# A scan kernel's last tile: one load in 32 KiB pieces in place of four loads in 2 KiB pieces, and three stores in place of four

## The chip, the cores and the metric

The kernel runs on one core of a Trainium2 chip. Times are device microseconds of one execution, unprofiled runs and a profiled one alike; the profile's *span* (from the first to the last recorded instruction of one profiled execution) is about 2 us shorter than the time.

The parts of a core that matter: TensorE (PE), VectorE (DVE), ScalarE (ACT), SyncE (SP, which here only issues loads), and 16 DMA engines that move all data between the chip's memory (HBM) and the on-chip memory (SBUF).

## The reference

`x` is 8 x 4096 x 2048 float32. Along the axis of 4096 the result is a running log-sum-exp:

```python
out[:, 0, :] = x[:, 0, :]
for t in range(1, S):
    mx = np.maximum(out[:, t-1, :], x[:, t, :])
    out[:, t, :] = mx + np.log(np.exp(out[:, t-1, :] - mx) + np.exp(x[:, t, :] - mx))
```

So 268.44 MB are read and 268.44 MB written, once each.

## The kernel before

A tile is 512 steps of one batch: 128 partitions, 4 successive rows each, 2048 columns. That is 4 MiB, and 32 KiB without a gap in HBM for each partition. There are 64 tiles, numbered 0 to 63 below, and five buffers. The columns of a tile are worked in four pieces of 512: ACT takes Exp, PE makes the prefix sums over the partitions, DVE adds the rows, ACT takes Ln. "Load 63" and "store 62" are the transfers of those tiles.

```python
    def load(b, k):
        t = iopool.tile([P, R, D], f32, name=f"io_{b}_{k}", tag="io")   # 5 buffers
        io[b, k] = t
        if (b, k) == tiles[-1]:
            for c in range(NC):                  # last tile: four column parts, runs of 2 KiB
                nc.sync.dma_start(out=t[:, :, cols(c)], in_=x_v[b, k][:, :, cols(c)])
        else:
            nc.sync.dma_start(out=t, in_=x_v[b, k])          # runs of 32 KiB
    ...
    def front(b, k, c):
        if c == 0:
            load(b, k)
        ...
        nc.scalar.activation(et, t[:, :, cols(c)], ACT.Exp)
    ...
    def back(b, k, c):
        t = io[b, k]
        nc.scalar.activation(t[:, :, cols(c)], sums.pop((b, k, c)), ACT.Ln)
        if (b, k) == tiles[-1]:
            nc.scalar.dma_start(out=o_v[b, k][:, :, cols(c)], in_=t[:, :, cols(c)])
        elif c == NC - 1:
            nc.scalar.dma_start(out=o_v[b, k], in_=t)

    for n, piece in enumerate(pieces):           # Ln of a piece comes two pieces after its Exp
        front(*piece)
        if n >= 1:
            carry(*pieces[n - 1])
        if n >= LAG:
            back(*pieces[n - LAG])
```

The softmax here doesn't subtract the row's maximum and nothing guards it: scores larger than these inputs give would overflow.

## Time and profile before

Median of four runs: 1259.86 us (1259.71 to 1260.11). The page of the profile begins so: the span, the busy time of each engine, the DMA share in 40 slices of the span (9 is 90% or more), and GB/s per slice:

```profile
span 1257.9 us, 5492 instructions
PE 638.5 (51%) x1472; PEld 215.0 (17%) x1472; DVE 703.3 (56%) x1024; ACT 930.0 (74%) x513; POOL 1.5 (0%) x10
DMA  9999999999999999999999999999999999999997
...
io<-in_x_dram SPq DMA_DIRECT2D x63, 4096.0 KB, 31.4
out_dram<-io ACTq DMA_DIRECT2D x63, 4096.0 KB, 38.5
io<-in_x_dram SPq DMA_DIRECT2D x4, 1024.0 KB, 39.4
out_dram<-io ACTq DMA_DIRECT2D x4, 1024.0 KB, 10.3
```

No compute engine is near full, and the DMA engines are: the kernel is bound by DMA. The last four lines are the DMA issues (number, size of one, median us from issue to landing).

The tail, in the timeline (start us, us, engine, line, operation, and in brackets how long the engine had been idle and what ended that):

```profile
1188.89 35.31 SPq L74 DMA_DIRECT2D io<-in_x_dram  x4
...
1199.57 24.63 SPq L74 DMA_DIRECT2D io<-in_x_dram  x1
...
1227.33 1.91 ACT L88 ACTIVATE et<-io 128x2048 bf16<-128x2048 f32 x1 [10.77 <-DMA io<-in_x_dram]
...
1234.67 0.34 ACTq L114 DMA_DIRECT2D out_dram<-io  x1
1246.97 0.54 ACTq L112 DMA_DIRECT2D out_dram<-io  x1
```

These are the four load issues of tile 63 (SP is held in them until 1224.2), its first Exp, the issue of store 62, and the last column store. The stretches view of the same time (stretch, length, busy us of each engine, TensorE clock, DMA share, GB/s):

```profile
1188.00:1202.00 14.00, 8.97 (x22) 3.02 (x21) 10.94 (x16) 14.00 (x8) 0.00 (x0) 0.80 1.00 422
1202.00:1220.00 18.00, 8.97 (x28) 3.11 (x27) 13.38 (x20) 14.55 (x9) 0.00 (x0) 1.00 1.04 431
1220.00:1236.00 16.00, 5.36 (x10) 1.76 (x10) 4.25 (x7) 8.67 (x5) 0.00 (x0) 0.57 0.48 183
1236.00:1258.00 22.00, 2.89 (x8) 0.78 (x7) 7.10 (x11) 9.55 (x6) 0.00 (x0) 0.54 0.91 358
```

From 1220 to 1236 the DMA engines are busy for 48%: 8.3 us of idle time for each engine *on average*.

The trace records when each DMA engine reports its share of a transfer as done, 16 reports for one transfer. I sorted these and took the median, the second latest and the latest engine (us; computed from the completion records, not a view of the profile):

```
before           median   second latest   latest    latest - median
tile  5 loaded     67.95        68.16       68.81       0.86
store 58         1180.23      1186.58     1188.84       8.61
store 60         1209.47      1213.33     1215.98       6.51
store 61         1223.58      1224.23     1226.36       2.78
load 63, part 4  1228.97      1232.42     1235.23       6.26
store 62         1245.86      1245.99     1246.59       0.73
last store       1256.73      1256.83     1256.95       0.22
```

One engine falls behind by some 8 us in the course of the run. All engines carry the same bytes of the tiles, and in the steady part none of them is idle. Others can run ahead because loads and stores are queued in advance. A tile is landed, and a buffer is free, only when the *latest* engine has reported. "DMA: Bandwidth & Descriptors" of the Trainium skill (Why a DMA increments its semaphore by 16 and not by 1) says the same: only the full count of 16 means that all data landed. The trace agrees: the next load is issued at 1188.89, 0.05 us after the latest engine's report for store 58, and 8.66 us after the median one's.

Besides the tiles, the DMA engines carry small transfers of the kind "instruction", which the page of the profile lists by queue (queue, kind: packets, MB, share of the engines' time):

```profile
q8 instruction: 11, 0.18, 0.1%
q14 instruction: 20, 0.16, 0.0%
```

In the steady part a packet starts when the one before it on its engine ends, so the packets of one engine can be followed as a chain. The chain of the latest engine holds eleven 8 KiB packets of queue 14, one about every 100 us from 57.8 to 1093.2 us; no other chain holds more than four. Each of them, with the stretched 32 KiB packet behind it (1.75 to 1.85 us in place of 1.21), costs the engine 0.85 to 0.94 us, 9.9 us together. Its other 32 KiB packets start every 1.210 us, as on the engines that are not late. The lag grows in steps, each after such a packet, and between the steps it is flat or falls (us; computed from the packet and completion records, not a view):

```
instruction packet at    latest - median before it    after it
 258.1                   1.75 (store 10)              2.76 (store 11)
 468.1                   3.58 (store 21)              4.49 (store 22)
 670.8                   4.23 (store 31)              5.19 (store 32)
 880.8                   6.00 (store 42)              6.97 (store 43)
1093.2                   7.79 (store 53)              8.75 (store 54)
```

So the latest engine is not slow as such: it has extra packets to carry. No run here changed the number of these packets, so this rests on the traces alone. The second latest engine is another case: its 32 KiB packets start every 1.219 us, and why stays open.

### The profile page before, as it was taken

To read this page: it belongs to the slowest core of one execution; us is meant where nothing else is said; L and a number is where in the kernel's file an instruction comes from. 1 tells how busy PE (TensorE), PEld (TensorE's weight loads), DVE (VectorE), ACT (ScalarE), POOL (GpSimd) and SP (SyncE) were. 2 spreads that over 40 slices of the span, in tenths; PEclk is the share of its full clock that TensorE was granted. 3 is DMA by queue.
4 is the path that set the end of the run, shared out by engine and by line. 5 is a ranking of instruction groups with operands and counts; after the bars stand their busy time and mean duration, and the time that the engine had idled before them with its cause. 6 is when DMAs were issued, how large, how long until landed. Compare 5 with 4: busy or idle time off the path is not lost.

```text
span 1257.9 us, 5492 instructions
## 1 busy us (share of the span) xinstructions
PE 638.5 (51%) x1472; PEld 215.0 (17%) x1472; DVE 703.3 (56%) x1024; ACT 930.0 (74%) x513; POOL 1.5 (0%) x10
## 2 busy tenths in 40 slices
PE   3655445544455455554556545455555454554542
PEld 1211112111111111111111111111111111111110
DVE  3665556565565554555555656565465555555453
ACT  5987768668677686776867768678687686776665
POOL 0000000000000000000000000000000000000000
PEclk9888688785887857878577786787767878678695
DMA  9999999999999999999999999999999999999997
GB/s 400 433 429 431 432 432 433 432 432 433 433 434 433 429 433 433 432 433 432 432 433 432 433 432 433 432 433 433 434 433 432 434 433 431 433 433 433 433 381 299
DMA packets 22399, 537.22 MB, mean 427 GB/s; under 512 B 2144, under 2 KB 2144, under 8 KB 6240
## 3 DMA queue, kind: packets, MB, share of 16 engines
q1 hardware_dynamic: 11184, 268.44, 49.7%
q10 hardware_dynamic: 11184, 268.44, 49.6%
q8 instruction: 11, 0.18, 0.1%
q14 instruction: 20, 0.16, 0.0%
HBM read 268.44 MB, written 268.44 MB: 427 GB/s over the span
## 4 chain that ended last, share of the span: by engine, by line
DMA 69%; ACT 14%; DVE 5%; PE 5%; issue 5%; SPq 1%; ACTq 0%; DVEq 0%
DMA io<-in_x_dram 67%; ACT io L110 8%; ACT et L88 5%; DVE st L98 4%; PE ps L91 3%; DMA out_dram<-io 2%; PE ps L103 2%; DVE st L96 1%; SPq L74 1%; ACTq L114 0%; ACTq L110 0%; DVEq L98 0%; ACTq L88 0%; DVEq L96 0%; SPq L76 0%
## 5 line engine op out<-in xcount | busy, mean ns | idle before, releaser
L88 ACT ACTIVATE et<-io 128x2048 bf16<-128x2048 f32 x256 | 485.3, 1897 | 301.1 <-DMA io<-in_x_dram 301.1
L98 DVE TENSOR_TENSOR st<-st,et 128x512 f32<-128x512 f32 x768 | 530.9, 692 | 43.4
L110 ACT ACTIVATE io<-st 128x2048 f32<-128x2048 f32 x256 | 484.6, 1894 | 15.0 <-DMA io<-in_x_dram 10.7
L96 DVE COPY st<-ps 128x512 f32<-128x512 f32 x256 | 176.7, 690 | 498.3 <-PE ps L91 492.9
L103 PE MATMUL ps<-st,last 128*128 128x512 f32 x448 | 304.6, 769 | 137.8 <-DVE st L98 136.6
L91 PE MATMUL ps<-et,Li 128*128 128x512 bf16 x256 | 124.9, 488 | 465.7 <-ACT et L88 463.9
L91 PE MATMUL ps<-et,Ls 128*128 128x512 bf16 x768 | 287.8, 497 | 0.0
L91 PEld LDWEIGHTS <-Ls 128*128 128x128 bf16 x768 | 89.4, 116 | 697.7 <-issue 668.1
L103 PEld LDWEIGHTS ps<-st,last 128*128 128x128 f32 x448 | 94.7, 234 | 250.8 <-DVE st L98 228.3
L91 PEld LDWEIGHTS <-Li 128*128 128x128 bf16 x256 | 30.8, 120 | 77.6 <-issue 70.2
L29 ACT ACT_TABLE_LOAD x1 | 1.3, 1283 | 0.8 <-PEq L138 0.8
masks.py:66 POOL TENSOR_SCALAR_AFFINE_SELECT Ls<-Ls 128x128 bf16<-128x128 bf16 x1 | 0.3, 293 | 0.0
L47 POOL TENSOR_SCALAR_AFFINE_SELECT last<-last 128x128 f32<-128x128 f32 x1 | 0.3, 292 | 0.1
masks.py:66 POOL TENSOR_SCALAR_AFFINE_SELECT Li<-Li 128x128 bf16<-128x128 bf16 x1 | 0.3, 292 | 0.0
masks.py:65 POOL MEMSET Ls<- 128x128 bf16 x1 | 0.2, 205 | 0.0
masks.py:65 POOL MEMSET Li<- 128x128 bf16 x1 | 0.2, 204 | 0.3 <-POOLq L138 0.3
L46 POOL MEMSET last<- 128x128 f32 x1 | 0.2, 204 | 0.0
L138 POOL MEMSET const-bfloat16-1.0<- 128x1 bf16 x1 | 0.1, 101 | 0.0
L138 POOL MEMSET const-uint8-127<- 128x1 uint8 x1 | 0.1, 101 | 0.0
L138 POOL MEMSET const-float32-0.0<- 128x1 f32 x1 | 0.1, 98 | 0.3 <-issue 0.3
L138 POOL MEMSET const-float32-1.0<- 128x1 f32 x1 | 0.1, 98 | 0.0
## 6 DMA issues: line engine op xcount, KB each, us to landing
io<-in_x_dram SPq DMA_DIRECT2D x63, 4096.0 KB, 31.4
out_dram<-io ACTq DMA_DIRECT2D x63, 4096.0 KB, 38.5
io<-in_x_dram SPq DMA_DIRECT2D x4, 1024.0 KB, 39.4
out_dram<-io ACTq DMA_DIRECT2D x4, 1024.0 KB, 10.3
```

Source lines behind the costliest of these rows:

```text
L29: nc.scalar.preload_act_table_set("natural_log_exp_and_others")
L46: nc.gpsimd.memset(last, 1.0)
L47: nc.gpsimd.affine_select(out=last, in_=last, compare_op=mybir.AluOpType.is_ge, fill=0.0, base=-(P - 1), pattern=[[0, P]], channel_multipl ...
L74: nc.sync.dma_start(out=t[:, :, cols(c)], in_=x_v[b, k][:, :, cols(c)])
L88: nc.scalar.activation(et, t[:, :, cols(c)], ACT.Exp)
L91: nc.tensor.matmul(ps, Li if r == 0 else Ls, et[:, r, :], start=(k == 0 and r == 0), stop=(r == R - 1), skip_group_check=True,)
L96: nc.vector.tensor_copy(st[:, 0, :], ps)
L98: nc.vector.tensor_add(st[:, r, :], st[:, r - 1, :], et[:, r, :])
L103: nc.tensor.matmul(bank(b, k + 1, c), last, sums[b, k, c][:, R - 1, :], start=True, stop=False, skip_group_check=True,)
L110: nc.scalar.activation(t[:, :, cols(c)], sums.pop((b, k, c)), ACT.Ln)
L138: nc = _bacc.Bacc("TRN2", target_bir_lowering=False, num_devices=1)
```

## The change

The intent was to give the last load the large pieces that all other loads have. The stores still leave in column parts, but the first two are joined to one of 1024 columns (runs of 4 KiB), so that there are three.

```diff
     def load(b, k):
         t = iopool.tile([P, R, D], f32, name=f"io_{b}_{k}", tag="io")
         io[b, k] = t
-        if (b, k) == tiles[-1]:
-            for c in range(NC):
-                nc.sync.dma_start(out=t[:, :, cols(c)], in_=x_v[b, k][:, :, cols(c)])
-        else:
-            nc.sync.dma_start(out=t, in_=x_v[b, k])
+        nc.sync.dma_start(out=t, in_=x_v[b, k])
@@ in back(), after the Ln
         if (b, k) == tiles[-1]:
-            nc.scalar.dma_start(out=o_v[b, k][:, :, cols(c)], in_=t[:, :, cols(c)])
+            if c > 0:
+                part = slice(0 if c == 1 else c * FD, (c + 1) * FD)
+                nc.scalar.dma_start(out=o_v[b, k][:, :, part], in_=t[:, :, part])
```

## The prediction

> **What bounds the kernel now.** DMA. The page's slices show the DMA engines 90% busy or more in 39 of 40 slices at 432 GB/s, while ACT, the busiest compute engine, is at 74%. The packet records of the trace give 1.213 us for a 32 KiB packet on one engine, loads and stores alike; each of the 16 engines has about 8 per tile and direction, so 63 loads and 63 stores are 1222.7 us of one engine's 1257.9 us span.
>
> **The tail before.** The timeline shows the last tile's four load issues from 1188.9 to 1224.2 us (35.3 us on SP; the fourth alone 24.6). Its first Exp starts at 1227.33, store 62 is issued at 1234.67, the last column store at 1246.97. Landings of the four parts: 1227.3, 1230.1, 1232.7, 1235.2. In the stretches view DMA is 48% busy from 1220 to 1236: summed over packets, 8.3 us idle per engine on average. The Trainium skill ("DMA: Bandwidth & Descriptors", Queues, rings and completion order) says that an engine goes round between queues packet by packet. The trace agrees: from 1214 to 1220 the load, in 2 KiB packets, gets about 11 GB/s and the 32 KiB stores 421.
>
> **The trap.** Recovering that 8.3 us would give 1250. But it is a mean. Completions per DMA (16 counts, one per engine) show one engine falling behind all through the run: 1.4 us behind the median at 100 us, 8.6 at 1188. That engine completes store 59 at 1205.6, store 60 at 1216.0, store 61 at 1226.4 (10.38 us = 8 x (1.213 + 0.084): one 2 KiB load packet between store packets), then the rest of its load packets until 1234.9. It idles only until store 62's first packets at 1235.5: 0.6 us. The chain is this engine's own queue; the idle 8.3 us belongs to the other fifteen.
>
> **What changes, on the slow engine.** Estimates from these durations:
> - load 63: 8 x 1.213 = 9.7 us in place of 128 x 0.084 = 10.75: -1.05
> - no gap before store 62: -0.6; store 62 without its slow restart (10.6 us for 8 packets there, 9.7 in steady state): about -0.6
> - the first store part in 4 KiB runs: about -0.25
>
> Sum -2.5. What moves but isn't on its path: the load shares 1:1 with stores 59 and 60 and lands whole at about 1221; Exp of the last tile starts about 1221.5, 6 us earlier, although all four parts now wait for the whole tile; store 62 is issued at about 1229, stores of the parts at 1236, 1238 and 1241. The slow engine has stores 60 and 61 until about 1234, store 62 until 1244: it never runs out, with some 5 us of slack, so the joined first store part and the coarser load cost nothing.
>
> **Prediction:** 1257.4 us, 80% range 1254.5 to 1259.6. Chances: faster by over 2% 0.01, within 2% 0.98, slower 0.01.
>
> **What would show it.** SP's issue under 1 us; the load landing at 1218-1223; no dip of the DMA share near 1225; in its place idleness at the very end: the last store's completion on the slowest engine several us after the median engine (before: 0.2 us). Last chain still DMA.
>
> **What would make it wrong.** If the slow engine's lag is caught up in the tail, or is smaller in unprofiled runs, the gain approaches the mean idle time (1250). If the load lands on the slow engine much later than 1225 (its packets not shared 1:1), store 62 comes after the queue runs dry and the gain goes, or it becomes slower by a few us. If the three column stores fill the queue and hold ACT, the last Ln is late, but that has about 10 us of slack.

## The result, and the profile after

1257.07 us, median of four runs (1256.90 to 1257.16). The ratio to before is 0.9977 (95% interval 0.996 to 0.9995): within 2%, and faster by 2.8 us. Ratios here are the mean time of one kernel's runs over that of the other's runs of the same rounds, so not quite the ratio of the medians. The page, with the same lines as above:

```profile
span 1255.4 us, 5457 instructions
PE 636.7 (51%) x1443; PEld 216.8 (17%) x1472; DVE 703.3 (56%) x1024; ACT 930.0 (74%) x513; POOL 1.5 (0%) x10
DMA  9999999999999999999999999999999999999997
...
io<-in_x_dram SPq DMA_DIRECT2D x64, 4096.0 KB, 31.4
out_dram<-io ACTq DMA_DIRECT2D x63, 4096.0 KB, 38.5
out_dram<-io ACTq DMA_DIRECT2D x1, 2048.0 KB, 13.2
out_dram<-io ACTq DMA_DIRECT2D x2, 1024.0 KB, 13.6
```

(The 29 missing PE instructions are matmul records lost from the trace; the weight loads are all there.) The timeline, the load issue, the first Exp of tile 63, store 62, the last column store:

```profile
1189.06 0.33 SPq L72 DMA_DIRECT2D io<-in_x_dram  x1
...
1221.56 1.91 ACT L84 ACTIVATE et<-io 128x2048 bf16<-128x2048 f32 x1 [4.87 <-DMA io<-in_x_dram]
...
1228.90 0.34 ACTq L113 DMA_DIRECT2D out_dram<-io  x1
...
1241.21 0.56 ACTq L111 DMA_DIRECT2D out_dram<-io  x1
```

The whole chain of compute moved forward by 5.8 us (first Exp 1227.33 to 1221.56, last store issue 1246.97 to 1241.21). The end moved by 2.5. The stretches:

```profile
1202.00:1220.00 18.00, 9.58 (x24) 3.37 (x24) 10.47 (x16) 14.51 (x8) 0.00 (x0) 0.85 1.00 433
1220.00:1236.00 16.00, 7.65 (x17) 2.48 (x17) 8.80 (x13) 14.44 (x9) 0.00 (x0) 0.64 0.74 317
1236.00:1258.00 22.00, 0.00 (x0) 0.00 (x0) 2.77 (x4) 3.78 (x3) 0.00 (x0) 0.51 0.63 246
```

The hole from 1220 to 1236 shrank from 48% busy to 74%, but the last stretch went from 91% to 63%. Summed over the packets, the idle time of an average engine was 8.3 us between 1220 and 1240 before; after it is 4.6 us there and 3.2 us from 1240 to the last packet, 7.8 together. Mean idleness hardly went; it moved. The completions show for whom:

```
after            median   second latest   latest    latest - median
store 58         1180.20      1186.44     1189.01       8.81
load 63          1211.70      1218.14     1221.48       9.78
store 60         1215.33      1221.77     1225.10       9.77
store 61         1225.01      1231.58     1234.76       9.75
store 62         1240.03      1241.39     1244.43       4.40
last store       1250.63      1251.32     1254.44       3.81
```

The latest engine goes from one transfer to the next without a stop: 9.66 us from its end of store 60 to that of store 61, 9.67 for store 62, which is 8 packets of 1.21 us each time. Fourteen engines wait for the compute between store 61 and store 62 and finish before it; the two latest do not wait.

The books of the latest engine, from the completions:

```
latest engine's stretch                          before    after   change
start of the run to store 58                    1188.84  1189.01   +0.17
store 58 to the end of all up to store 61
   and load 63                                    46.39    45.75   -0.64
from there to the end of store 62                 11.36     9.67   -1.69
the last tile's stores                            10.36    10.01   -0.35
sum                                             1256.95  1254.44   -2.51
```

The span went from 1257.9 to 1255.4 us, by 2.5.

One caution for the column "before": down to load 63 the latest engine is the same one, but at store 62, when all engines start afresh together, the latest report (1246.59) comes from another engine, which had an instruction packet at 1244.46. The fifteen others had reported by 1245.99. So how the last two changes divide is uncertain; their sum, -2.04, is not.

### The profile page after: what moved, and what is told of

It is laid out like the page before. It is cut to its first block, busy times and chain, and to the rows that moved or that the text cites. A ratio compares the mean times of both kernels' runs of the same rounds, so it can differ in the third digit from the quotient of the medians. Undisturbed runs are those within 1.5% of the kernel's fastest.

```text
span 1255.4 us, 5457 instructions
## 1 busy us (share of the span) xinstructions
PE 636.7 (51%) x1443; PEld 216.8 (17%) x1472; DVE 703.3 (56%) x1024; ACT 930.0 (74%) x513; POOL 1.5 (0%) x10
## 4 chain that ended last, share of the span: by engine, by line
DMA 69%; ACT 14%; DVE 5%; PE 5%; issue 5%; ACTq 0%; another core or an unknown queue 0%; DVEq 0%; SPq 0%
DMA io<-in_x_dram 67%; ACT io L106 9%; ACT et L84 5%; DVE st L94 4%; PE ps L87 3%; DMA out_dram<-io 2%; PE ps L99 2%; DVE st L92 1%; ACTq L106 0%; DVEq L94 0%; ACTq L113 0%; ACTq L84 0%; DVEq L92 0%; SPq L72 0%
## 5 line engine op out<-in xcount | busy, mean ns | idle before, releaser
L87 PE MATMUL ps<-et,Ls 128*128 128x512 bf16 x739 | 280.5, 500 | 1.6 <-issue 1.1
## 6 DMA issues: line engine op xcount, KB each, us to landing
out_dram<-io ACTq DMA_DIRECT2D x1, 2048.0 KB, 13.2
```

The lines of the kernel that those rows point to most:

```text
L87: nc.tensor.matmul(ps, Li if r == 0 else Ls, et[:, r, :], start=(k == 0 and r == 0), stop=(r == R - 1), skip_group_check=True,)
```

## The experiments

**Theory.** One DMA engine, slower than the rest, is the bound of the whole program. The time is what its own queue takes. The change gained what it took off that queue.

**Rivals.** (1) Mean DMA throughput is the bound, so extra bytes cost in proportion to all 16 engines. (2) The chain of compute behind the last load is the bound, and its earlier start is the gain. (3) The number of transfers or buffer turns cost.

Eleven kernels ran, all correct. All times are medians; "before" in the same rounds was 1259.92, 1259.65 and 1259.70 us in the three timed groups, so times of different groups can be compared within some 0.3 us.

| run | time, us | against the changed kernel (1257.07) |
|---|---|---|
| e1_load_only | 1257.50 | +0.4 |
| e2_store_only | 1259.62 | +2.6 |
| e3_whole_store | 1256.93 | -0.1 |
| e4_skip15_mid | 1272.66 | +15.6 |
| e5_delay2 | 1258.08 | +1.0 |
| e5_delay7 | 1270.58 | +13.5 |
| e6_extra7 | 1261.04 | +4.0 |
| e6_extra8 | 1260.87 | +3.8 |
| e7_probe (one look) | 1258.37 | (before beside it: 1260.39) |
| e8_extra3 | 1257.44 | +0.4 |
| e8_extra4 | 1261.10 | +4.0 |

### The two halves of the change, one at a time

The load half alone, with before's four column stores (against the changed kernel):

```diff
-            if c > 0:
-                part = slice(0 if c == 1 else c * FD, (c + 1) * FD)
-                nc.scalar.dma_start(out=o_v[b, k][:, :, part], in_=t[:, :, part])
+            nc.scalar.dma_start(out=o_v[b, k][:, :, cols(c)], in_=t[:, :, cols(c)])
```

> The one-DMA load alone, with the four 2 KiB column stores of before. Theory (the slowest DMA engine's own queue is the bound): the load part is nearly all of the gain; this run is 0.3 to 0.5 us slower than the changed kernel (1257.07), that is 1257.4 to 1257.6, because the last tile's store is 64 packets of 2 KiB more in place of 32 of 4 KiB on that engine. Rival (the earlier start of the last tile's compute chain is the gain): the same as the changed kernel or slightly faster, since the first column now leaves one piece earlier: 1256.5 to 1257.1.

Measured: 1257.50 us (1257.13 to 1258.05). In the trace the latest engine needs 10.17 us for the last tile's four stores (1245.09 to 1255.26), against 10.01 for three in the changed kernel. This is what the theory said; but the 0.4 us to the changed kernel is little more than the 0.3 us by which groups differ.

The store half alone, with before's four loads (against before):

```diff
-            nc.scalar.dma_start(out=o_v[b, k][:, :, cols(c)], in_=t[:, :, cols(c)])
+            if c > 0:
+                part = slice(0 if c == 1 else c * FD, (c + 1) * FD)
+                nc.scalar.dma_start(out=o_v[b, k][:, :, part], in_=t[:, :, part])
```

> The joined first store part alone, with the four-part 2 KiB load of before. Theory: 0.3 us faster than before, 1259.5. Rival (the joined store leaves 3.6 us later than the first column did and so costs overlap): 1 to 3 us slower than before.

Measured: 1259.62 us (1259.30 to 1260.20), 0.3 faster than before in the same rounds (1259.92), with an interval of the ratio that holds 1 (0.9983 to 1.0013). The load is 2.4 of the 2.8 us; the store is a few tenths, which these rounds can't tell from nothing. Leaving 3.6 us later cost the first column nothing.

### No column parts at all

```diff
-            if c > 0:
-                part = slice(0 if c == 1 else c * FD, (c + 1) * FD)
-                nc.scalar.dma_start(out=o_v[b, k][:, :, part], in_=t[:, :, part])
+            if c == NC - 1:
+                nc.scalar.dma_start(out=o_v[b, k], in_=t)
```

> The changed kernel with the last tile stored as one DMA of 32 KiB packets after its last Ln (at about 1241.2 us). Theory: the slowest engine is busy with store 62 until 1244.1, so a store issued at 1241.2 still finds it busy, and it needs 9.7 us in place of 10.0 for the last tile: 0.3 us faster than the changed kernel, 1256.8; the last store's completion on the slowest engine still 2 to 3 us after the median. Rival (the column parts are worth their overlap of compute and store): the fast engines wait from 1240 to 1242, and the whole is 1.4 us slower or more, 1258.5.

Measured: 1256.93 us (1256.43 to 1257.88), span 1255.1. The latest engine ends store 62 at 1244.62 and the last store at 1254.26, 9.64 us later, and 1.79 us after the median. So storing the last tile whole, which gives up every overlap of its compute with its stores, costs nothing: those engines that would have used the overlap are not the bound. The difference of 0.1 to the changed kernel is too small to call; this is the simplest of the three programs and not slower.

### Delay of the last tile's compute

```diff
-        nc.scalar.activation(et, t[:, :, cols(c)], ACT.Exp)
+        for _ in range(3 if (b, k, c) == pieces[-NC] else 1):    # 8 in the second run
+            nc.scalar.activation(et, t[:, :, cols(c)], ACT.Exp)
```

> The changed kernel with the first Exp of the last tile done three times over (two extra, 1.8 us each, just after the load lands), so that store 62 and all of the last tile's stores are issued 3.6 us later. Theory (the slowest DMA engine has stores queued until 1234.4, store 62 was issued at 1228.9 and starts 0.8 us after issue): no change, 1257.1 within 0.3. Rival (the compute chain that follows the last load is the bound, as the chain of waits lists it): 3.6 us slower, 1260.7.

> The same with seven extra Exp, 12.6 us of delay. Theory: the slack of 4.7 us is used up, the rest shows: 7.9 us slower, and up to 1 us more for the restart of the idle engine, 1265 to 1266. Rival: 12.6 us slower, 1269.7. In the trace, completions of the last store within 0.5 us of each other on all engines, as all start afresh together.

Measured: 1258.08 us (+1.0) and 1270.58 us (+13.5). Neither number is the one I wrote, in either theory, and the timeline shows why: the builder of the program did not keep the extra Exp in one place, but moved the Ln of tile 62 ahead of some of them. The delay fell more on the last tile's stores than on store 62. With two extra Exp, here store 62, the first two column stores and the last one:

```profile
1232.79 0.34 ACTq L114 DMA_DIRECT2D out_dram<-io  x1
...
1242.85 2.34 ACTq L112 DMA_DIRECT2D out_dram<-io  x2
...
1247.95 0.56 ACTq L112 DMA_DIRECT2D out_dram<-io  x1
```

Store 62 was issued 3.9 us later than in the changed kernel (1228.90), and the DMA share from 1220 to 1236 fell as low as before the change:

```profile
1220.00:1236.00 16.00, 7.04 (x14) 2.21 (x15) 3.77 (x8) 12.70 (x7) 0.00 (x0) 0.53 0.46 199
```

Yet the latest engine ended store 62 at 1244.71, 0.28 us later, and 0.30 of that had been there at store 58 already (1189.31 against 1189.01). This is the clean part of the run: a larger hole for the other engines, and nothing lost. The extra 1 us came afterwards: the joined first part was issued 6.7 us later (1242.85 in place of 1236.10), when all engines were starting afresh, and took the latest engine 6.06 us in place of 4.88. With seven extra Exp the first part was issued at 1255.22, 11 us after the latest engine had ended store 62 (1244.15), and the completions of the last store lie within 0.2 us of each other, as expected of engines that all restart together. The +13.5 alone lies nearer to the rival's 12.6 than to the theory's 8 to 9; but the last store was issued 18.5 us later than in the changed kernel (1259.68 against 1241.21) and landed only 13.2 us later (1267.68 against 1254.44), so some 5 us of the delay were absorbed. So there is slack of several microseconds, and beyond it the delay of the compute chain shows. The forecast sizes (+0 and +8 to 9) assumed where the delay would fall, and were wrong for that reason.

### Which engine it is: a try that failed

The Trainium skill ("DMA: Bandwidth & Descriptors", Why a DMA increments its semaphore by 16 and not by 1) says how many engines a transfer uses: the largest number up to 16 that divides its rows, and of the 16 the lowest-numbered ones. It also says (Latency and other measured facts) that engines 7 and 15 are usually the slower ones; its best guess at a cause concerns DMAs issued from GpSimd, and this kernel issues all of its own from SP and ACT. A load of 120 rows leaves engine 15 out:

```diff
+        if (b, k) == tiles[40]:
+            nc.sync.dma_start(out=t[:120], in_=x_v[b, k][:120])
+            nc.sync.dma_start(out=t[120:], in_=x_v[b, k][120:])
+        else:
-        nc.sync.dma_start(out=t, in_=x_v[b, k])
+            nc.sync.dma_start(out=t, in_=x_v[b, k])
```

> The changed kernel with the load of tile 40 split into partitions 0 to 119 (15 engines of 8 rows, the last engine left out) and 120 to 127 (8 engines of one row): takes one tile's 9.7 us of load from engine 15, gives engines 0 to 7 one packet (1.2 us) more. Theory: one engine is the bound. If it is engine 15, the second slowest engine (2.6 us less behind at 1189 us) bounds instead: 2.6 us faster, 1254.5 (1.4 faster, 1255.7, if the second one is among 0 to 7). If the slowest is among 0 to 7: 1.2 us slower, 1258.3. If among 8 to 14: no change. Rival (mean DMA bandwidth and the tail's compute chain bound): no change in any case, as the bytes and the tail are the same.

Measured: 1272.66 us (1271.09 to 1273.32), 15.6 slower than the changed kernel. No theory of mine allowed this. The stretches of this run, with the load of tile 40 in flight in the second:

```profile
720.00:740.00 20.00, 11.02 (x27) 3.88 (x26) 11.63 (x18) 15.16 (x10) 0.00 (x0) 0.80 0.99 426
740.00:780.00 40.00, 12.96 (x32) 4.27 (x31) 18.69 (x28) 21.64 (x12) 0.00 (x0) 0.69 1.00 370
780.00:820.00 40.00, 20.80 (x46) 7.10 (x46) 22.04 (x32) 29.02 (x16) 0.00 (x0) 0.71 1.01 432
```

and of the changed kernel in the second:

```profile
740.00:780.00 40.00, 18.97 (x42) 6.36 (x43) 22.77 (x34) 30.34 (x18) 0.00 (x0) 0.67 1.00 433
```

The engines were busy all the time and moved 370 GB/s in place of 433: single packets took longer (a 32 KiB load packet 1.61 us on average between 742 and 778 us, against 1.21 in the changed kernel). The same page of the Trainium skill (The descriptor swizzle) says that in a transfer over 128 partitions each engine writes one port of SBUF. With 120 rows that match is gone, which may be the cause; no run here shows it. The run says nothing about engine 15, as its cost hides any gain. Of the 15.6 us only 5.8 are the hole itself (63 of 433 GB/s for 40 us); the rest came with a wider spread of the engines afterwards, and stays open.

### Extra work on some engines only

To load chosen engines without this, extra *stores* were put behind store 50, of few rows, four partitions apart, 32 KiB each, to places of the last tile's output that are overwritten at the end. With three such stores an engine that takes part has three packets more, 3 x 1.213 = 3.6 us, and the others nothing.

```diff
         elif c == NC - 1:
             nc.scalar.dma_start(out=o_v[b, k], in_=t)
+            if (b, k) == tiles[50]:
+                bl, kl = tiles[-1]
+                for j in range(3):              # 4*n with n = 7 rows here; 8, 3 and 4 in other runs
+                    nc.scalar.dma_start(
+                        out=o_v[bl, kl][:28].rearrange("(e j) r d -> e j r d", j=4)[:, j],
+                        in_=t[:28].rearrange("(e j) r d -> e j r d", j=4)[:, j])
```

> The changed kernel with three more stores after that of tile 50, each of 7 rows of 32 KiB (places of the last tile that are overwritten later), which by the rule for choosing engines go to engines 0 to 6 alone: 3.6 us of work more for each of these. Theory: if the slowest engine isn't among them, no change (under 0.3 us), since the other engines have 6 us to spare at that point; if it is, 3.6 us slower. Rival (mean DMA throughput is the bound): 7/16 of 3.6, 1.6 us slower, 1258.7.

> The same with 8 rows each, engines 0 to 7: one engine more, the one that the Trainium skill says is usually among the slower. Theory: if engine 7 is the slowest, 3.6 us slower, 1260.7; if it is the second slowest (2 to 2.6 us ahead of the slowest), about 1.2 us slower; if neither, no change. Rival (mean): 1.8 us slower, 0.2 more than with 7 rows.

Measured: 1261.04 us (1260.77 to 1261.52) and 1260.87 us (1260.81 to 1261.30). Seven engines with 3.6 us of work more cost 4.0, the eighth nothing more. So the slowest engine is among 0 to 6, and it is not engine 7. But rival (3), that three more transfers cost by their number, would give the same. The completions of the first extra store, one for each engine that took part, say more (us):

```
7 rows:  1026.1  1026.2  1028.6  1030.2  1030.3          1034.4  1037.2
8 rows:  1027.4  1027.4  1027.5  1028.6  1028.6  1030.3  1034.3  1036.6
```

With 7 rows the two late engines are there already. To find their numbers, six tiny stores of 1 to 6 rows:

```diff
+            for at, first in ((48, 1), (52, 4)):
+                if (b, k) == tiles[at]:
+                    bl, kl = tiles[-1]
+                    for e in range(first, first + 3):
+                        j, r = (e - 1) % 4, (e - 1) // 4
+                        nc.scalar.dma_start(
+                            out=o_v[bl, kl][:4 * e].rearrange("(e j) r d -> e j r d", j=4)[:, j, r, :FD],
+                            in_=t[:4 * e].rearrange("(e j) r d -> e j r d", j=4)[:, j, r, :FD])
```

> The changed kernel with six tiny extra stores of 1 to 6 rows of 2 KiB behind the stores of tiles 48 (1, 2, 3 rows) and 52 (4, 5, 6 rows), which run on engines 0 to k-1 alone and queue behind those engines' own packets: their completions tell which engine lags. Theory: one of engines 0 to 6 lags 8 us behind the median, another 5 us (in the run with three times 7 extra rows, two of seven completions came 4.1 and 6.9 us after the fifth); the first k whose completions include one that is late names it. The time does not change, 1257.1. Rival (the lag is not one engine's, but moves from engine to engine with each DMA): the late completions come with no fixed k, and may show with k = 1.

Measured: one run of 1258.37 us beside one of before at 1260.39. The probes were not free of effect: ACT waited up to 12 us to issue one. Their completions, beside the two latest engines of the store that was ahead of them in the queue (us):

```
probe     completions                                  two latest of the store ahead
1 row     968.1                                         972.3   974.5
2 rows    987.6  990.4                                  991.8   994.8
3 rows    987.4  990.1  992.8                           991.8   994.8
4 rows   1044.4 1045.9 1051.0 1055.4                   1050.2  1052.9
5 rows   1063.8 1064.1 1071.1 1072.2 1077.3            1069.7  1074.8
6 rows   1066.3 1066.6 1067.5 1072.6 1074.7 1078.8     1069.7  1074.8
```

A probe that comes directly behind that store is done up to 2.5 us after it on the same engine, and never before it (the probe of 6 rows stands behind the one of 5 as well). With 1 to 3 rows no completion is as late as the latest engine (974.5, 994.8). With 4 rows one is, 2.5 us after it (1055.4 after 1052.9); with 5 rows a second late one appears (1072.2 after 1069.7). So the slowest is the fourth engine in the order of rows, number 3 by the skill's rule, and the second slowest number 4. That gives the test which all theories must answer differently:

> As with 7 extra rows, but 3 rows in each of the three extra stores: engines 0 to 2 alone, 3.6 us of work more for each of these. The probe run showed none of these three as one of the two late ones (the fourth engine, number 3, was the latest, number 4 the second). Theory: no change against the changed kernel, 1257.1 within 0.4. Rival (three more stores in the queue cost by their number, or hold the buffer of tile 50): 3.5 us or more slower, as with 7 and 8 rows. Rival (mean): 0.7 us slower.

> The same with 4 rows: engine 3 added, 98 KB more than with 3 rows. Theory: engine 3 is the bound of the whole kernel, so its 3 packets of 1.213 us show in full: 3.6 us slower, 1260.7. Rival (number of stores): the same as with 3 rows. Rival (mean): 0.2 us more than with 3 rows.

Measured: 1257.44 us (1257.29 to 1257.61) with engines 0 to 2, and 1261.10 us (1260.86 to 1262.66) with engine 3 added. Three engines with 3.6 us more work each cost 0.4 us at most, within what was allowed; three packets on a fourth engine cost 3.7 us more. The number of transfers is the same in both. The DMA issues on the two pages differ in one line, 96 KB for each extra store, then 128 KB:

```profile
span 1255.7 us, 5461 instructions
...
out_dram<-io ACTq DMA_DIRECT2D x3, 96.0 KB
```

```profile
span 1259.1 us, 5461 instructions
...
out_dram<-io ACTq DMA_DIRECT2D x3, 128.0 KB
```

and the completions show the engine that was added, and where it ends:

```
                  first extra store                    last store: 2nd latest, latest
engines 0 to 2    1027.4  1027.4  1030.3                1252.06  1254.70
engines 0 to 3    1026.2  1027.4  1030.4  1036.9        1252.13  1258.10
```

98 KB of 537 MB in the wrong place, 0.02%, cost 3.7 us; three times as much on three other engines cost nothing that stands out. Rivals (1) and (3) fall with this pair, and rival (2) with the whole store and with the delayed store 62, as far as the slack reaches. Before the change the slack was used up: the latest engine ended its last load packet at 1234.9 and store 62's first packets started at 1235.5, so there an earlier start of the compute did gain something.

## Why the prediction was right

- **The time.** 1257.4 was predicted, with 1254.5 to 1259.6 as the range; 1257.07 was measured. The step it hung on, that one engine's queue is the bound and the mean idle time is not, is shown by the pair with 3 and 4 rows. The prediction did not say why this engine lags, and did not need to; it is the instruction packets in its queue that the traces show.
- **The terms of the sum.** Predicted -2.5 in all; the latest engine's books give -2.51. Inside the sum there were wrong sizes that made up for each other, so its closeness is in part luck. Large packets in the load were put at -1.05 and gave -0.64: I took 0.084 us for a 2 KiB packet, its recorded length, but packets back to back start every 0.080 us. Some 109 of the 128 were back to back and 19 alternated with store packets, so 109 x 0.080 + 19 x 0.084 = 10.3 us, and 10.3 - 9.7 = 0.6. The gap before store 62, its slow restart and the stores of the last tile were put at -1.45 together and gave -2.04. The 10.6 us that the prediction took for the slow engine's restart were those of the other engine with the instruction packet at 1244.46. So most of the gain on the latest engine is not the larger load packets (0.64) but what comes after them, above all the gap and the common restart, which an earlier store 62 avoided. Up to store 58, which the change doesn't touch, the profiled run was 0.17 us later.
- **What moved without gain.** Load 63 was to land at about 1221 (1221.48), SP's issue to take under 1 us (0.33), store 62 to be issued at about 1229 (1228.90), the column stores at 1236, 1238 and 1241 (first 1236.10, last 1241.21). All held.
- **One sign to look for was wrong.** "No dip of the DMA share near 1225": it is still there, 74% busy from 1220 to 1236. I had reckoned stores 60 and 61 for the slow engine, which has them until 1234, and forgot that the fast ones, some 10 us ahead, are through with them at about 1225 and then wait for store 62, which is issued at 1228.9. Idleness at the very end did come as said: the latest engine reports 3.8 us after the median, before 0.2.
- **Slack.** Some 5 us were claimed for store 62. It was issued 3.9 us late in one run and nothing was lost; beyond the slack, the run with seven extra Exp lost 13.5.

## What to carry to other kernels

A DMA share of 48% in the tail is a mean over 16 engines, and a transfer is done when the last of them is. Before counting idle DMA time as a gain, look at the spread of the completions of single transfers: if one engine lags, what can be gained is its own idle time and the work that a change takes off it. Then ask what that engine carries besides the tiles: here it was some 0.9 us for each instruction packet, eleven times. And a late start of the compute at the end costs nothing as long as the slowest engine still has stores queued.

## What the Trainium skill lacked or had wrong

- "DMA: Bandwidth & Descriptors", Latency and other measured facts: engines 7 and 15 are named as usually slower. The page's best guess at a cause concerns DMAs issued from GpSimd, and there are none here. Engine 7 was not the slowest: by the rule for choosing engines on the same page, engine 3 was the latest and engine 4 the next (with 4 rows one completion came 6.5 us after the rest, with 5 rows a second late one appeared), and adding engine 7 to engines 0 to 6 changed nothing (1260.87 against 1261.04 us).
- No page says what instruction packets cost the tile transfers that share their DMA engine: here 0.85 to 0.94 us for each 8 KiB packet on the latest engine. They add up, 0.86 us behind the median at 68 us and 8.61 at 1189 us, and then this engine sets the end of the program.
- "DMA: Bandwidth & Descriptors", Queues, rings and completion order (one packet from each queue in turn): the runs agree, and the consequence is worth stating. From 1214 to 1220 us six engines sent one 2 KiB load packet and one 32 KiB store packet in turn, and the load got 11 GB/s of 432; the ten others had no load packet to send.
- The same page, Issuing engines are not separate DMA queues: issue time is called usually small relative to the DMA itself. The fourth 1 MiB load of 2 KiB runs held SP for 24.63 of the 35.66 us from its issue to its landing; the 4 MiB load of 32 KiB runs takes 0.33.
- The same page, Use all 16 engines (Rules for kernel authors): it advises an outermost size that is a multiple of 16, which 120 rows are not, but gives no figure for what 15 engines cost. One load of 120 rows brought the rate from 433 to 370 GB/s for 40 us, and the whole run lost 15.6 us; the cause is open.
